# Two gate pairs moved behind the last attention scores, with earlier output weights split over DVE and POOL

## The chip, the core and the metric

The kernel runs on one NeuronCore of a Trainium2 chip. The metric is the device time of one launch in microseconds (us), taken as the median of the runs. The core has five engines that run side by side: TensorE (PE, the matrix array), VectorE (DVE), ScalarE (ACT), GpSimd (POOL) and SyncE (SP, which here only issues DMAs). Each engine works through its own list of instructions in order. An instruction whose operand is not ready stops everything behind it on that engine.

## The reference, cut to what matters

One layer: a norm, one input projection, two mixers on the same normalised input (causal pooling, and latent attention with a mask by chunks of 64 tokens), one output projection, the residual, and a final norm.

```python
u = rmsnorm(h, norm_g) @ w_in
pool_in, pool_gate, c_q, c_kv, k_r, attn_gate = split(u)
pool_out = silu(pool_gate) * pool_mixer(pool_in, pool_w, pool_scale)
q = rmsnorm(c_q) @ w_q_b ; kv = rmsnorm(c_kv) @ w_kv_b
s = (q_nope . k_nope + q_rope . k_rope) * scale      # chunk c sees keys of chunks <= c
attn = softmax(mask(s)) @ v
attn_out = silu(attn_gate) * attn
h = h + concat(pool_out, attn_out) @ w_out
return rmsnorm(h, final_norm_g)[:, 16:]
```

There are 16 meta tokens and 2048 tokens, a model width of 1024, 4 heads, 512 pooling channels and 512 attention channels.

## The kernel before

**Attention.** The 32 chunks of 64 queries are taken one by one in an order written out by hand (`seq`). The stretch that matters here runs over the chunks 19, 18, ..., 8. For a chunk c and a pair of heads p (0 or 1), `scores(c, p)` computes each block of keys with five matmuls into a PSUM bank of the tag "s" (L433 to L437; six such banks). DVE takes the row maxima (L439, L444, L445), ACT the exponentials (L460) and a half-precision copy (L463, L468), DVE or POOL the remainder that the copy lost (L465, L469), and SP issues a DMA that transposes the result into a tile pt (L472), one DMA for each page of keys. `pv(c)` multiplies pt by the values (L496, three matmuls for each tile of keys) into a bank o. It is called one chunk behind the scores: `step(c, 1, 1)` computes the scores of chunk c and then the values of the chunk before it. After four chunks `vproj` (L520, L521) makes an attention tile `at` of 256 tokens.

**The other mixer and the gates.** The 256-token blocks are numbered i = 0 to 7. `load_w(pi)` loads the raw weights of pair pi (L577) and takes their absolute sums on ACT (L580). `scale_w(pi)` finds a power of two by a small matmul (`wmx`, L80) and DVE (L81 to L88), and splits the scaled weights into two half-precision parts (ACT L597, L599, L600; DVE L598; POOL L601). `load_x(i)` does the like for the input of block i (SP L564, DVE L566, ACT L569, POOL L570). `pair(i, pi)` runs two projections of 24 matmuls each (`mproj`, L613) with a gate behind each (ACT L644, L648; DVE L649). Pairs 4 and 5 hold the attention gates (weights 8, 9 and 10, 11), and their result is multiplied into the attention tile on POOL (L702). Pairs 0 to 3 hold a pooling group (`pool_in`: ACT L622, DVE L628, L633, ACT L637 writes `plh`, DVE L638 writes `pll`) and its gate; `pool_out` (three matmuls L658) is put one pair later.

**Output.** `load_wo(k)` loads 128 rows of the output weights (L680) and splits them into a high part (ACT L681) and a low part (DVE L682). `op_prep(t)` makes the two-part operands `mh` (ACT L718, L719) and `ml` (POOL L720, DVE L721) of 128 tokens and loads the residual `xr` (L723). `op(t)` runs 2 x 24 matmuls of 512 columns (L738), adds the residual, norms and stores.

**What sets the order.** The code's own order is a table: `FILL` names the chunks behind which a gate pair is put (after c = 15, 13 and 11, taken from the list `fill` of L805), `PREP` the chunks behind which weights and inputs are loaded, and `TAIL` everything after the attention ("24" is `pair(2, 4)`, "b3" `scale_w(3)`, "o5" `load_wo(5)`, "p0" `op_prep(0)`, "x3" `load_x(3)`). A list scheduler of the framework then merges these into one list for each engine. All raw loads (`raw`, L545: weights, inputs, output weights, residual) share two buffers of one tag, so that a load can be issued when the load two places ahead of it has been used up.

```python
FILL = {15: 1, 13: 1, 11: 1}                                  # L46
return cpools[0].tile([P, cols], F32, name=name, tag="wr", bufs=2, padded_shape=[P, 1088])   # L548
nc.vector.tensor_sub(out=t[:, 1], in0=wr, in1=f(t[:, 0]))     # L682
fill = [(0, 4), (0, 5), (1, 4)]                               # L805
```

## Time and profile before

| | |
|---|---|
| runs | 906.87, 904.96, 903.70 us |
| median | 904.96 us |
| the profiled execution: time, span | 908.45 us, 906.7 us |
| PE busy | 859.5 us (95%) |
| DVE, ACT, POOL busy | 509.3, 455.3, 328.4 us |
| PE idle between 350 and 465 us | 14.07 us |
| PE idle between 465 and 600 us | 7.65 us |
| PE idle between 600 and 850 us | 0 us |

Times inside the execution are counted from the span's start. "Granted clock" is the share of full speed that PE was given: 1.00 is 2.4 GHz, 0.50 is 1.2 GHz. A row of the waits names the waiting instruction, the engine and instruction that it waited for, and how much in total, how often and the longest. In a timeline, the number in brackets at a row's end is the idle time before it and what ended it.

### The profile page before, as it was taken

The page shows a single profiled execution, that of the slowest core. Times are in us where ns is not written, and L with a number is a line of the kernel's source. Part 1 is how long each engine was busy: PE and PEld are TensorE (multiplying, and loading weights), DVE is VectorE, ACT ScalarE, POOL GpSimd, SP SyncE. Part 2 cuts the span into 40 slices and gives each one's busy share as a digit, 9 for nine tenths or more (in the row PEclk, how much of TensorE's full clock was granted, in tenths as well). Part 3 has the DMA queues.
Part 4 walks back from the last instruction along what each step waited for, and adds up shares of the span by engine and source line. Part 5 has one row for each costly group of instructions (what it writes and reads, how often), then busy time and mean ns, then how long its engine had stood idle before and what let it go on. Part 6 is the DMA issues. An engine that isn't in the chain of part 4 may idle for free. (4 is left out here: it accounts for less than half of the span.)

```text
span 906.7 us, 16178 instructions
## 1 busy us (share of the span) xinstructions
PE 859.5 (95%) x5849; PEld 747.1 (82%) x5849; DVE 509.3 (56%) x1224; ACT 455.3 (50%) x1189; POOL 328.4 (36%) x520
## 2 busy tenths in 40 slices
PE   9799899999999999898989997999999999999996
PEld 8699778889888888777878885888888888888885
DVE  5377678756667757768624678454442532534322
ACT  6576657747668667677625554332322312213221
POOL 2566553434545434536413223331312312312020
PEclk9899999999999999998999999999999999999999
DMA  7756525886898788965932234231311312310011
GB/s 267 209 180 176 145 49 103 157 152 131 141 148 146 125 174 138 177 133 141 173 76 74 78 117 145 70 95 72 102 47 47 101 46 64 100 47 1 24 47 70
DMA packets 206955, 101.79 MB, mean 112 GB/s; under 512 B 169257, under 2 KB 196363, under 8 KB 206875
## 3 DMA queue, kind: packets, MB, share of 16 engines
q1 hardware_dynamic: 187392, 93.30, 43.4%
q10 hardware_dynamic: 19483, 7.47, 3.9%
q8 instruction: 46, 0.75, 0.4%
q14 instruction: 34, 0.28, 0.1%
HBM read 55.60 MB, written 8.43 MB: 71 GB/s over the span
## 5 line engine op out<-in xcount | busy, mean ns | idle before, releaser
L613 PEld LDWEIGHTS <-w 128*128 128x128 f16 x2304 | 222.0, 98 | 35.8 <-issue 7.2
L613 PE MATMUL mp<-xx,w 128*128 128x256 f16 x2016 | 233.0, 274 | 0.0
L738 PE MATMUL op<-wo,mh 128*128 128x512 f32 (+1 forms) x528 | 161.3, 388 | 3.1 <-ACT mh L718 3.1
L465 POOL TENSOR_TENSOR hl<-p,hl 128x512 f16<-128x512 f32 (+4 forms) x104 | 102.7, 1008 | 107.0 <-ACT hl L463 102.4
L460 ACT ACTIVATE p<-s,st 128x512 f32<-128x512 f32 (+8 forms) x168 | 99.2, 600 | 52.7 <-DVE st L445 44.0
L738 PEld LDWEIGHTS op<-wo,mh 128*128 128x128 f32 x528 | 97.1, 188 | 23.6 <-ACT mh L718 3.4
L496 PE MATMUL o<-pt,vh 128*128 128x256 f16 x544 | 92.6, 274 | 5.2 <-DMA pt<-hl 4.8
L439 DVE TENSOR_REDUCE st<-s 128x1 f32<-128x512 f32 (+6 forms) x154 | 88.2, 587 | 14.9 <-PE s L437 14.0
L463 ACT CAST hl<-p 128x512 f16<-128x512 f32 (+6 forms) x168 | 82.3, 541 | 5.6 <-DMA pt<-hl 4.3
L740 DVE TENSOR_TENSOR xr<-op,xr 128x512 f32<-128x512 f32 (+1 forms) x33 | 22.2, 674 | 104.3 <-PE op L738 104.3
L496 PE MATMUL o<-pt,vl 128*128 128x256 f16 x272 | 74.5, 274 | 0.0
L742 ACT ACTIVATE osq<-xr 128x512 f16<-128x512 f32 (+1 forms) x33 | 20.4, 618 | 106.7 <-DVE xr L740 97.1
L496 PEld LDWEIGHTS <-vh 128*128 128x128 f16 x544 | 51.9, 98 | 15.1 <-DMA pt<-hl 4.4
L644 ACT ACTIVATE th<-mp,whalf 128x256 f32<-128x256 f32 x64 | 30.1, 471 | 54.4 <-PE mp L613 52.4
L738 PE MATMUL op<-wo,ml 128*128 128x512 f32 x144 | 56.6, 395 | 0.0
L570 POOL TENSOR_TENSOR xx<-yr,xx 128x512 f16<-128x512 f32 x28 | 35.3, 1277 | 45.3 <-ACT xx L569 45.3
L465 DVE TENSOR_TENSOR hl<-p,hl 128x512 f16<-128x512 f32 (+7 forms) x64 | 43.5, 681 | 13.6 <-ACT hl L463 12.5
L433 PE MATMUL s<-klo,qh 128*128 128x512 f32 (+9 forms) x116 | 44.8, 386 | 4.5 <-ACT gt L648 3.4
L623 POOL COPY carry<-u 128x16 f32<-128x16 f32 x32 | 15.2, 475 | 85.2 <-ACT u L622 85.2
L738 PE MATMUL op<-wo,ml_odd 128*128 128x512 f32 (+1 forms) x120 | 45.5, 379 | 0.0
L566 DVE SCALAR_TENSOR_TENSOR yr<-yr,gxs,rbc 128x256 f32<-128x256 f32 (+1 forms) x64 | 32.9, 573 | 21.1 <-DMA yr<-hT_in 17.4
L702 POOL TENSOR_TENSOR at<-at,gt 128x256 f32<-128x256 f32 x32 | 23.5, 734 | 55.7 <-DVE gt L649 45.2
(216 smaller groups left out, 1884.3 us busy)
## 6 DMA issues: line engine op xcount, KB each, us to landing
xt<-hcat_in SPq DMA_DIRECT2D x16, 512.0 KB, 5.3
xr<-hcat_in SPq DMA_DIRECT2D x16, 512.0 KB, 3.6
raw<-hT_in SPq DMA_DIRECT2D x15, 512.0 KB, 5.0
out_dram<-xr SPq DMA_DIRECT2D x15, 512.0 KB, 2.6
yr<-hT_in SPq DMA_DIRECT2D x14, 512.0 KB, 3.7
wr<-w_m_in SPq DMA_DIRECT2D x12, 512.0 KB, 4.5
rb<-rd ACTq DMA_DIRECT2D x32, 128.0 KB, 4.5
wor<-w_out_in SPq DMA_DIRECT2D x8, 512.0 KB, 3.9
```

What stands on the lines that cost most here:

```text
L433: nc.tensor.matmul(ps[:, :w], lhsT=q(qh), rhs=kt[:, 0, 0, sl], start=True, stop=False)
L439: nc.vector.reduce_max(out=mx[:, bi:bi + 1], in_=ps[:, :w], axis=AX.X)
L460: nc.scalar.activation(out=pr[:, o:o + w], in_=pss[bi][:, :w], func=AF.Exp, bias=nb_, accum_out=sm[:, bi:bi + 1] if nb > 1 else tot)
L463: nc.scalar.copy(out=hl[:, 0, sl], in_=pr[:, sl])
L465: eng.tensor_tensor(out=hl[:, 1, sl], in0=pr[:, sl], in1=hl[:, 0, sl], op=ALU.subtract)
L496: nc.tensor.matmul(ps[:, :2 * P], lhsT=v, rhs=x, start=i == 0, stop=i == len(ops) - 1)
L566: nc.vector.scalar_tensor_tensor(out=xr[:, k - k0], in0=xr[:, k - k0], scalar=gxs[:, k:k + 1], in1=rbc, op0=ALU.mult, op1=ALU.mult)
L570: nc.gpsimd.tensor_tensor(out=xl[:, k:k + 2], in0=xr[:, k - k0:k - k0 + 2], in1=xh[:, k:k + 2], op=ALU.subtract)
L613: nc.tensor.matmul(ps[:, :n - sk], lhsT=a[:, k], rhs=x[:, k, sk:n], start=e == 0, stop=e == 3 * KT - 1)
L644: nc.scalar.activation(out=th, in_=ps[:, :G], func=AF.Tanh, scale=whalf[:, wts[m][2]:wts[m][2] + 1])
L702: nc.gpsimd.tensor_tensor(out=t[:, m - 8], in0=t[:, m - 8], in1=gt, op=ALU.mult)
L738: nc.tensor.matmul(ps[:, :w], lhsT=x[:, k], rhs=y[:, sl], start=i == 0, stop=i == 3 * KT - 1)
```

## The change

- The gate pairs (0, 4) and (0, 5) are put behind the chunks 16 and 14 instead of 15 and 13.
- The pair (1, 4) is taken out of the attention loop (it was behind chunk 11), and (1, 5), which was the pair "15" of the tail, joins it: both follow the last scores, with the values of the last chunk, 8, between them.
- In the tail, `scale_w(3)` stands ahead of the pair (1, 1), the output weights 0 to 5 are each loaded one pair sooner, and `op_prep(0)` stands ahead of `load_x(3)` instead of behind the output weights 6.
- The low part of the output weights is made half on DVE (columns 0 to 511) and half on POOL (columns 512 to 1023).

```diff
-FILL = {15: 1, 13: 1, 11: 1}
+FILL = {16: 1, 14: 1}
-TAIL = """b0 w a1 15 24 b1 25 a2 00 10 b2 20 a3 01 11 b3 21 o0 02 o1 12 o2 22 o3 03 o4 13 o5 x3 23 o6 p0 o7 g
+TAIL = """b0 w a1 24 b1 25 a2 00 10 b2 20 a3 01 b3 11 o0 21 o1 02 o2 12 o3 22 o4 03 o5 13 p0 x3 23 o6 o7 g
-        nc.vector.tensor_sub(out=t[:, 1], in0=wr, in1=f(t[:, 0]))
+        nc.vector.tensor_sub(out=t[:, 1, :512], in0=wr[:, :512], in1=f(t[:, 0, :512]))
+        nc.gpsimd.tensor_tensor(out=t[:, 1, 512:], in0=wr[:, 512:], in1=f(t[:, 0, 512:]), op=ALU.subtract)
-    fill = [(0, 4), (0, 5), (1, 4)]
+    fill = [(0, 4), (0, 5), (1, 4), (1, 5)]
+    while fill:
+        pair(*fill.pop(0))
+        if pend:
+            pv(pend.pop(0))
     flush()
-    while fill:
-        pair(*fill.pop(0))
```

In the lists below, `s8_1_1` is the second block of keys of chunk 8 and head pair 1, `o9` the values of chunk 9, `mp1_10` the projection of block 1 with weights 10, `wmx0` the scaling of the tail's first weights, `p15_...` the exponentials of chunk 15.

PE, from the last matmul of the last scores to the scaling of the tail's first weights, before (each row stands for a run of equal rows; weight loads are left out):

```order
L437 MATMUL s8_1_1_6025<-klo_115,qr2_4921 128x336
L613 MATMUL mp1_10_6167<-xx_5318,w10_5150 128x256
L496 MATMUL o10_5963<-pt10_1_5825,vh_120 128x256
L613 MATMUL mp1_11_6197<-xx_5318,w11_5156 128x256
L496 MATMUL o9_6056<-pt9_0_5917,vh_120 128x256
L613 MATMUL mp2_8_6229<-xx_5318,w8_4738 128x256
L496 MATMUL o8_6075<-pt8_0_6006,vh_120 128x256
L496 MATMUL o8_6075<-pt8_1_6014,vh_120 128x256
L613 MATMUL mp2_9_6259<-xx_5318,w9_4744 128x256
L80 MATMUL wmx0_6125<-ident_84,wmx_108 128x128 x4
```

The same place now:

```order
L437 MATMUL s8_1_1_5963<-klo_115,qr2_4982 128x336
L613 MATMUL mp1_8_6013<-xx_5318,w8_4738 128x256
L496 MATMUL o11_5799<-pt11_0_5640,vh_120 128x256
L496 MATMUL o10_5901<-pt10_0_5755,vh_120 128x256
L613 MATMUL mp1_9_6043<-xx_5318,w9_4744 128x256
L613 MATMUL mp1_10_6116<-xx_5318,w10_5212 128x256
L496 MATMUL o9_5994<-pt9_0_5855,vh_120 128x256
L496 MATMUL o8_6075<-pt8_0_5944,vh_120 128x256
L613 MATMUL mp1_11_6146<-xx_5318,w11_5218 128x256
L613 MATMUL mp2_8_6229<-xx_5318,w8_4738 128x256
L80 MATMUL wmx0_6187<-ident_84,wmx_108 128x128 x4
```

The first gate projection of block 1 and the values of chunk 11 have moved behind the last scores. Ahead of the first matmul of `o8` there now stand 57 gate and 53 value matmuls; before, there were 51 and 25. From the last scores to `wmx0` there are 111 gate, 68 value and 12 `av` matmuls; before, 109, 40 and 12.

ACT, around the input cast of block 0 (L569), the exponentials of chunk 15 (L460) and the absolute sums of weights 10 (L580), before:

```order
L597 ACTIVATE w9_4744<-wr9_4593,wsc_104 128x512
L460 ACTIVATE p15_0_0_5015,st15_0_4990<-s15_0_0_4992,st15_0_4990 128x384
L600 CAST w8_4738<-wr8_4587 128x512
L460 ACTIVATE p15_1_0_5064,st15_1_5040<-s15_1_0_5041,st15_1_5040 128x384
L569 CAST x0_4750<-yr0_0_4753 128x544 x2
L580 ACTIVATE wa10_0_4905,wmx_108<-wr10_4903 128x512
L460 ACTIVATE p14_0_0_5241,st14_0_5224<-s14_0_0_5225,st14_0_5224 128x512
```

And now:

```order
L597 ACTIVATE w9_4744<-wr9_4593,wsc_104 128x512
L600 CAST w8_4738<-wr8_4587 128x512
L569 CAST x0_4750<-yr0_0_4753 128x544
L580 ACTIVATE wa10_0_4905,wmx_108<-wr10_4903 128x512
L644 ACTIVATE th0_8_4941<-mp0_8_4915,whalf_106 128x256
L644 ACTIVATE th0_9_4971<-mp0_9_4945,whalf_106 128x256
L460 ACTIVATE p15_0_0_5077,st15_0_5052<-s15_0_0_5054,st15_0_5052 128x384
```

The exponentials of chunk 15 have moved behind the input of block 0, the loads of weights 10 and 11, and the gates of the pair (0, 4).

SP, the raw loads at the end of the output weights, before:

```order
L680 DMA wor5_7284<-w_out_in 128x1024
L564 DMA yr3_0_7290<-hT_in 128x4x256
L564 DMA yr3_4_7300<-hT_in 128x4x256
L680 DMA wor6_7388<-w_out_in 128x1024
L723 DMA xr0_7398<-hcat_in 128x1024
L680 DMA wor7_7401<-w_out_in 128x1024
```

And now:

```order
L680 DMA wor5_7212<-w_out_in 128x1024
L724 DMA xr0_7300<-hcat_in 128x1024
L564 DMA yr3_0_7304<-hT_in 128x4x256
L564 DMA yr3_4_7314<-hT_in 128x4x256
L680 DMA wor6_7402<-w_out_in 128x1024
L680 DMA wor7_7408<-w_out_in 128x1024
```

The residual `xr0` has moved ahead of the two halves of the input of block 3. It keeps its raw buffer until the first output rows are stored, so the four loads behind it take turns in the other one.

## Rows read from the trace of the kernel before

**Rows 1.** Busy time by stretch: length, PE, PEld, DVE, ACT, POOL; clock; DMA share, GB/s.

```profile
650.00:850.00 200.00, 200.00 (x1419) 170.94 (x1418) 80.86 (x167) 53.55 (x123) 46.96 (x74) 1.00 0.17 57
```

**Rows 2.** The same view, ahead of and behind the end of the last scores.

```profile
358.60:447.90 89.30, 79.36 (x576) 70.76 (x575) 65.13 (x170) 61.47 (x172) 44.22 (x58) 0.96 0.77 158
447.90:471.50 23.60, 19.48 (x163) 16.54 (x162) 7.14 (x18) 7.22 (x21) 4.82 (x9) 0.93 0.56 96
```

**Rows 3.** The same view: two stretches of slow clock, and the tail.

```profile
416.00:423.00 7.00, 6.42 (x23) 5.77 (x24) 5.53 (x14) 5.21 (x15) 5.57 (x7) 0.52 0.45 117
...
460.50:464.00 3.50, 3.44 (x18) 2.53 (x19) 0.00 (x0) 0.00 (x0) 0.00 (x0) 0.55 0.26 50
...
500.00:600.00 100.00, 92.35 (x693) 78.03 (x691) 67.69 (x132) 45.67 (x94) 27.61 (x42) 1.00 0.32 99
```

**Rows 4.** PE's waits from 350 to 465 us: total, times, longest.

```profile
PE o L496 <- DMA pt<-hl: 4.1, 1, 4.1
PE s L433 <- ACT gt L648: 3.4, 1, 3.4
```

**Rows 5.** PE's timeline at the last scores: start, length, instruction, count.

```profile
447.49 0.40 PE L437 MATMUL s<-klo,qr 128*128 128x336 f32 x1
...
448.83 4.31 PE L613 MATMUL mp<-xx,w 128*128 128x256 f16 x38
...
454.97 1.47 PE L613 MATMUL mp<-xx,w 128*128 128x256 f16 x12
460.56 0.61 PE L496 MATMUL o<-pt,vh 128*128 128x256 f16 x2 [4.12 <-DMA pt<-hl]
```

**Rows 6.** ACT's timeline from 365 to 452 us, seven rows of it.

```profile
365.35 0.57 ACT L460 ACTIVATE p<-s,st 128x384 f32<-128x384 f32 x1
...
384.70 0.67 ACT L460 ACTIVATE p<-s,st 128x512 f32<-128x512 f32 x1
...
403.65 1.14 ACT L600 CAST w<-wr 128x512 f16<-128x512 f32 x2
...
415.17 0.62 ACT L569 CAST xx<-yr 128x512 f16<-128x512 f32 x1 [0.17 <-DVE yr L566]
...
416.42 0.58 ACT L460 ACTIVATE p<-s,st 128x384 f32<-128x384 f32 x1
...
437.16 0.58 ACT L460 ACTIVATE p<-s,st 128x384 f32<-128x384 f32 x1 [3.33 <-issue]
...
451.11 0.20 ACT L460 ACTIVATION_READ_ACCUMULATOR p<-s,st 128x1 f32 x1
```

**Rows 7.** SP's timeline: half of block 2's input, and the last twelve transposes.

```profile
421.08 0.52 SPq L564 DMA_DIRECT2D yr<-hT_in  x1
...
440.19 17.55 SPq L472 DMA_TRANSPOSE pt<-hl  x12
```

**Rows 8.** PE's waits from 465 to 600 us.

```profile
PE op L738 <- ACT mh L718: 3.1, 1, 3.1
PE pm L658 <- ACT plh L637: 2.1, 1, 2.1
PE wmx L80 <- ACT wa L580: 1.5, 2, 1.1
PE pm L658 <- DVE pll L638: 1.0, 1, 1.0
```

**Rows 9.** Groups on DVE and POOL, 500 to 600 us: count, busy, mean ns, idle.

```profile
L682 DVE TENSOR_TENSOR wo<-wor,wo 128x1024 fp32r<-128x1024 f32 x8 | 9.8, 1223 | 8.8 <-ACT wo L681 8.8
...
L601 POOL TENSOR_TENSOR w<-wr,w 128x512 f16<-128x512 f32 x4 | 4.8, 1200 | 4.0 <-ACT w L600 4.0
```

**Rows 10.** DVE's timeline: a `pl` beside a POOL subtraction, and one without.

```profile
554.26 1.38 DVE L633 SCALAR_TENSOR_TENSOR pl<-w,u 128x256 f32<-128x256 f32 x1
...
561.78 0.42 DVE L633 SCALAR_TENSOR_TENSOR pl<-w,u 128x256 f32<-128x256 f32 x1
```

**Rows 11.** DMA issues, 500 to 575 us: count, size, median us to landing.

```profile
yr<-hT_in SPq DMA_DIRECT2D x2, 512.0 KB, 3.7
```

## The prediction

> **What bounds the kernel now.** I read busy time by stretch first, then PE's waits in the stretches where PE is not full, and last the timelines of the engines that it waits for. From 650 to 850 us PE is busy 200.00 of 200.00 us [rows 1]: there the time is PE's work, the change neither adds nor takes a matmul, and nothing can be won. All that can move is PE's idle time and slow clock ahead of 600 us.
>
> Three terms make that loss. Ahead of the end of the last scores, from 358.60 to 447.90 us, PE is idle 89.30 - 79.36 = 9.94 us, and from 416 to 423 us it runs at a granted clock of 0.52, the lower level of 1.2 GHz, right after a wait of 3.4 us [rows 2 to 4], which costs 7.00 x 0.48 = 3.4 us more: 13.3 us together. Behind the last scores, from 447.90 to 471.50 us (the scaling `wmx0` of the tail's first weights), PE is idle 4.12 us, all of it one wait of `o8` for the transposed softmax of chunk 8 [rows 2, 4, 5], and in the 3.5 us behind that wait its clock is 0.55 [rows 3], which costs 1.6 us: 5.7 us together. In the tail from 500 to 600 us it is idle 100.00 - 92.35 = 7.65 us [rows 3], in four kinds of waits [rows 8].
>
> **The change part by part.** First the two pairs behind the last scores. The need: the last score ends at 447.85 us (the row at 447.49 and its 0.40), and the last page of pt is there when `o8` starts at 460.56 [rows 5]: 12.7 us later. The cover: a gate matmul takes 0.109 us (38 from 448.83 to 452.98, their 4.31 less the overlap with the next [rows 5]), and a value matmul about the same. Before, 51 gate and 25 value matmuls stood between, 76 x 0.109 = 8.3 us; now 57 and 53, 110 x 0.109 = 12.0 us. So 0.7 us of wait is left at most, if the last pages come no later against the last score than now; I take 0.5, and with so short a wait no slow clock (the one of 3.4 us was followed by it). This term falls from 5.7 to 0.5.
>
> What has been moved there is missing ahead. 48 gate and 28 value matmuls are gone from before the last scores, 76 x 0.109 = 8.3 us, and PE's busy time there (79.36 less the 3.4 us of slow clock, 76.0) falls to 67.7. That alone would bring the last scores to 439.6 if the loss of 13.3 us stayed. It does not stay by itself, since the softmax sets the pace. The exponentials of chunk 15 were at 365.35, ahead of block 0's input; in the new list they stand behind it, behind the loads of weights 10 and 11 and behind the gates of (0, 4), all of which used to come behind them. A gate of (0, 4) needs block 0's whole input and 48 matmuls, so I put them at about 383, just ahead of where chunk 14's were (384.70 [rows 6]). From there ACT has one chunk more to do than before. Two things that it did later are already done (the gates of (0, 4) and the absolute sums of weights 10 and 11). The scaling of weights 10 and 11 then ends near 395 instead of 403.65, the first input cast group of block 1 ends 12 us behind it (403.65 to 415.17 [rows 6]), and block 2's, which now stands ahead of chunk 12's exponentials on ACT, another 11 us on: its raw loads need block 1's buffers, and each takes a landing of 3.7 us [rows 11], the scaling on DVE and the casts. So chunk 12's exponentials start at about 418.5, against 416.42 before.
>
> From there on no load is left in between. From 437.16 to 451.31 ACT did three chunks [rows 6] in 14.15 us with three absolute sums of 0.72 each among them, so 4.0 us a chunk; five chunks and the issue of the four reciprocal DMAs (3.3 us [rows 6]) take 23.5 us and end at 442.0. The last exponential ended 3.5 us behind the last score (451.31 against 447.85), so the last score would end at 438.5. PE must stand still for part of this, about 5 us ahead of chunk 11's scores, whose banks wait for chunk 12's exponentials, and the row of 3.4 us says that the lower clock follows: 2 us. With 3.2 us up to 381 (about as now), 1.5 for the scaled weights 10 and 2.0 for the late pt of chunk 15, the loss ahead is 13.7 us, and the last scores end at 358.6 + 67.7 + 13.7 = 440.0. The bounds: 10 us if the slow clock and half of the bank wait do not come (the idle time of now without its slow clock), 20 if block 2's second half is held up as it was before (421.08, behind a transpose on the same queue [rows 7]).
>
> Behind the last scores come 111 gate, 68 value and 12 `av` matmuls, 191 x 0.11 = 21.0, so that `wmx0` stands at 461.5. Before it stood at 471.5 with 46 more gate matmuls done, 5.0 us; on equal work 466.5. **Gain 13.3 + 5.7 - 13.7 - 0.5 = 4.8 us**, bounds -2 and 9.
>
> The tail. `wmx0` now stands 81 gate matmuls ahead of block 0's first pooling projection, 8.9 us, where it stood 35 ahead; so the chain of raw loads (weights 1, 2, 3, then the output weights) runs some 5 us earlier against PE, and the output weights are one pair sooner for that reason, not at a cost. The wait for `mh`, 3.1 us [rows 8], goes: between the two pooling outputs ahead of `op(0)` all 48 matmuls of the pair (2, 3) stand in one piece, 5.2 us, and `mh` is asked for behind them. In its place come others. The casts of output weights 3, 4 and 5 stand on ACT and DVE ahead of block 2's and 0's `plh`: I count 0.7, 3.3 and 1.1 us for the last three `pm` where 2.1 and 1.0 were [rows 8]. The serial raw buffer adds a new pair: input of block 3, first half, second half, output weights 6, 7, each issued only when POOL has finished with the one before, some 7 us a link (3.7 landing [rows 11], DVE 1 to 2, a cast, 1.2 on POOL [rows 9]); 6 is ready about 1.7 us and 7 about 0.7 us behind PE. The scaling waits stay at about 1.2 of 1.5. Sum 8.7 against 7.65: **loss 1.0 us**, bounds -5 and +2 (6 would be the present waits with only the `mh` wait halved; 12.5 if each link is 1.5 us longer).
>
> Splitting the low part: DVE's 1.22 us becomes about 0.65, POOL gets eight times 1.2 [rows 9]. The buffer is free when the slower is done, 1.2 behind the cast as before, so nothing is won on the chain, and POOL (27.61 of 100 us busy [rows 3]) has room. But a `pl` that ran beside a POOL subtraction took 1.38 us, and one without it 0.42 [rows 10]; that may make single links longer and is in the bound above. The Trainium skill's page "SBUF — State Buffer" (section "Who interferes with whom") says that a DVE instruction with two SBUF inputs and a GpSimd instruction that reads SBUF exclude each other for their whole length. By that rule, which speaks against this split and which the 1.38 us agrees with, DVE's and POOL's halves would run one after the other, 1.85 us instead of 1.22, about 0.6 us on each of the three links up to block 3's input, and the sum of the tail would be a loss of some 3 us instead of 1.
>
> Together 4.8 - 1.0 = 3.8 us: 908.45 becomes 904.65. The profiled execution lies 3.5 us (0.4%) above the median of 904.96; the difference carried over to the median gives 901.2.
>
> **The rivals.** *The whole gap goes.* If block 1's and 2's inputs come through as fast as their engines allow, the loss ahead is 10 us and not 13.7, and the tail stays at 7.65: 8.7 us gained, 896. For it: ACT is busy only 61.47 of 89.30 us there, DVE 65.13 [rows 2], so neither is full. Against it: the loads and the softmax stand in one list, and every landing stops the exponentials behind it.
>
> *Exchange.* The wait in front of `o8` comes back ahead, or part of it stays: the last twelve transposes took 17.55 us of SP's queue, 1.46 each [rows 7]. From 420.5 on twenty are due and two weight loads, 30 us, the last landing near 454, while PE reaches `o8` at 440.0 + 12.0 = 452.0. With 2 us left there, and 15 instead of 13.7 ahead, the gain is 2.0 and the tail takes 1.0: 904.
>
> *Slower.* One mechanism: chunk 12's exponentials wait on ACT for the last cast of block 2, in a list that cannot be overtaken. Each of its two halves can be issued only when POOL has freed the buffer, behind whatever stands on SP. If that is 8 us later than I count, the last scores end at 448; on equal work the tail starts 448 + 21.0 + 0.5 - 466.5 = 3.0 us late, plus 1.0 from the tail, and an idle stretch of over 10 us ahead brings 1 us more of slow clock: 5 us lost, 910. It decides once the last scores end after 444, four us behind my figure, with the tail's 1.0 counted.
>
> That the change does not do what it says is no rival: the order of instructions shows both pairs behind the last scores.
>
> **How the numbers follow.** A difference under about 0.3%, 2.7 us, can't be told from no change here. Forecast 0.45, 901.2 with an own range of 899 to 904, a quarter of it inside the 0.3%; whole gap 0.17, 896; exchange 0.16, 904; slower 0.22, 910. Faster 0.34 + 0.17 = 0.51; same 0.11 + 0.16 = 0.27; slower 0.22. The range runs from 895 to 909.5, which leaves out the lower part of the second case and half of the last, about 0.2.
>
> **What would show it.** Right: the wait of `o8` for pt under 1 us and no clock of 0.55 behind it; chunk 15's exponentials near 383, chunk 12's near 418, last scores near 440; no wait for `mh`, new waits of `op` for output weights 6 and 7 (L681), longer `pm` waits. Wrong: last scores after 444, a wait at `o8` over 2 us, a wait of over 3 us in the scores of chunks 13 to 8 in more than one place, or raw loads of the output weights more than 7 us apart on each buffer.

## The result, and the profile after

The change makes the kernel slower: 911.52 us (median of 12 runs) against 906.50 us, ratio 1.0055, interval 1.0035 to 1.0076, so about +5 us where -3.8 us was forecast. The profiled executions are 911.58 and 908.45 us, a difference of 3.1 us; single executions of one kernel differ by several us here, so ratios carry the verdicts and the traces the reasons. A difference of two ratios below is uncertain by about 0.3%.

Two views of the changed kernel answer to [rows 2] and [rows 4]: busy time by stretch (length, PE, PEld, DVE, ACT, POOL; clock, DMA share, GB/s), cut at the end of the last scores (443.30) and at `wmx0` (468.23), with a stretch in which PE mostly stands (418 to 422) and the slow clock behind it; then PE's waits from 350 to 470 us.

```profile
358.44:443.30 84.86, 72.82 (x499) 63.78 (x498) 64.88 (x163) 56.95 (x154) 42.37 (x53) 0.94 0.71 146
443.30:468.23 24.93, 21.25 (x193) 18.60 (x191) 7.83 (x23) 11.11 (x35) 6.17 (x13) 1.00 0.74 140
418.00:422.00 4.00, 1.14 (x7) 0.81 (x6) 4.00 (x6) 3.84 (x11) 4.00 (x4) 1.00 0.12 33
422.00:426.00 4.00, 2.81 (x10) 2.20 (x10) 4.00 (x13) 2.15 (x6) 4.00 (x4) 0.60 0.94 180
```

```profile
PE s L433 <- ACT p L460: 5.2, 3, 2.9
PE o L496 <- DMA pt<-hl: 3.7, 2, 2.8
PE qt L361 <- POOL qra L357: 1.8, 1, 1.8
```

Ahead of the last scores PE is idle 12.0 us and loses 84.86 x 0.06 = 5.1 us more to the clock (some 0.9 us of that fall into idle time and are counted twice): 17.1 us, where 13.3 were before. Behind them it is idle 3.7 us with no slow clock, where 5.7 us were lost. The wait for pt [rows 4, 5] was to go; 3.7 of 4.1 us of it are still there. New are 5.2 us of waits of the scores for exponentials (1.1 us in the kernel before).

What it waits for is on SP. SP's timeline: the two halves of block 2's input, then the transposes and two weight loads up to the last one; and the two rows of PE that wait for the two pages of chunk 8.

```profile
409.49 3.90 SPq L564 DMA_DIRECT2D yr<-hT_in  x2
...
420.92 23.59 SPq L472 DMA_TRANSPOSE pt<-hl  x16
444.56 1.05 SPq L577 DMA_DIRECT2D wr<-w_m_in  x2
446.03 11.64 SPq L472 DMA_TRANSPOSE pt<-hl  x8
```

```profile
458.24 0.39 PE L496 MATMUL o<-pt,vh 128*128 128x256 f16 x2 [2.81 <-DMA pt<-hl]
...
460.70 0.39 PE L496 MATMUL o<-pt,vh 128*128 128x256 f16 x2 [0.87 <-DMA pt<-hl]
```

From 420.92 to 457.67 SP does nothing but 24 transposes and two loads: 1.47 us for each transpose, without a gap. The last ones end at 457.7; before, the last row of twelve ended at 440.19 + 17.55 = 457.7 too [rows 7]. The matmuls were moved, the end of this queue was not. ACT's timeline shows why 24 were due, those of chunks 13 to 8: chunk 15's exponentials are at 386.75, chunk 13's at 414.22, behind block 1's input, and chunk 12's at 421.15. In the kernel before (the last row here) chunk 13's were at 395.98, ahead of that input.

```profile
386.75 0.58 ACT L460 ACTIVATE p<-s,st 128x384 f32<-128x384 f32 x1 [0.29 <-DVE st L445]
...
414.22 0.69 ACT L460 ACTIVATE p<-s,st 128x512 f32<-128x512 f32 x1 [2.53 <-DMA rbc<-rd]
...
421.15 0.59 ACT L460 ACTIVATE p<-s,st 128x384 f32<-128x384 f32 x1
```

```profile
395.98 0.69 ACT L460 ACTIVATE p<-s,st 128x512 f32<-128x512 f32 x1 [1.60 <-DVE st L445]
```

In the tail the wait for `mh` [rows 8] is gone. PE's waits from 470 to 650 us, and the clock behind the longest:

```profile
PE pm L658 <- ACT plh L637: 3.3, 2, 3.0
PE op L739 <- ACT wo L681: 1.5, 2, 1.3
PE pm L658 <- DVE pll L638: 1.2, 1, 1.2
PE op L739 <- POOL wo L683: 0.2, 1, 0.2
```

```profile
547.00:550.00 3.00, 2.55 (x17) 2.09 (x18) 1.87 (x5) 1.25 (x3) 0.40 (x2) 0.84 0.26 91
550.00:555.00 5.00, 5.00 (x36) 3.88 (x33) 4.91 (x8) 2.29 (x6) 4.44 (x3) 0.75 0.12 21
```

The waits are 6.2 us in all where 7.7 were, but behind the wait of 3.0 us at 547.45 the clock falls to 0.84 and 0.75, 3.00 x 0.16 + 5.00 x 0.25 = 1.7 us; before, the clock was 1.00 there [rows 3]. Rows of DVE, POOL and PE up to that wait:

```profile
540.15 0.69 DVE L682 TENSOR_TENSOR wo<-wor,wo 128x512 fp32r<-128x512 f32 x1 [1.39 <-ACT wo L681]
...
540.76 1.52 DVE L628 TENSOR_TENSOR w<-u 128x287 f32<-128x287 f32 x1
```

```profile
540.20 1.78 POOL L683 TENSOR_TENSOR wo<-wor,wo 128x512 fp32r<-128x512 f32 x1 [3.04 <-ACT wo L681]
```

```profile
546.54 0.41 DVE L633 SCALAR_TENSOR_TENSOR pl<-w,u 128x256 f32<-128x256 f32 x1
```

```profile
547.45 0.39 PE L658 MATMUL pm<-plh,pwh 128*128 128x256 f32 x1 [2.98 <-ACT plh L637]
```

POOL's half begins at 540.20, beside DVE's half, and ends at 541.98; DVE's next operation with two inputs takes 1.52 us, where the same operation takes 0.45 in kernel 3 below, which has nothing on POOL there, and ends 0.3 us behind POOL. So the two halves and the operation behind them run one after another: 0.69 on DVE, some 1.1 more on POOL, then DVE again. Each of the six weights that came ahead of 547 us held DVE up by about a microsecond in this way, some half a microsecond more than the half of the subtraction that it was spared, and DVE's `pl` at 546.54 is what the wait goes back to.

### The profile page after: what moved, and what is told of

It is laid out like the page before. It is cut to its first block, busy times and chain, and to the rows that moved or that the text cites. A ratio compares the mean times of both kernels' runs of the same rounds, so it can differ in the third digit from the quotient of the medians.

```text
span 909.8 us, 16209 instructions
## 1 busy us (share of the span) xinstructions
PE 864.2 (95%) x5849; PEld 749.2 (82%) x5849; DVE 515.5 (57%) x1224; ACT 456.9 (50%) x1189; POOL 342.4 (38%) x528
## 5 line engine op out<-in xcount | busy, mean ns | idle before, releaser
L613 PE MATMUL mp<-xx,w 128*128 128x256 f16 x2016 | 230.5, 274 | 0.0
L460 ACT ACTIVATE p<-s,st 128x512 f32<-128x512 f32 (+8 forms) x168 | 99.4, 601 | 53.0 <-DVE st L445 45.0
L741 DVE TENSOR_TENSOR xr<-op,xr 128x512 f32<-128x512 f32 (+1 forms) x33 | 22.3, 675 | 101.8 <-PE op L739 101.8
L496 PEld LDWEIGHTS <-vh 128*128 128x128 f16 x544 | 52.1, 98 | 14.9 <-DMA pt<-hl 4.2
L465 DVE TENSOR_TENSOR hl<-p,hl 128x512 f16<-128x512 f32 (+7 forms) x64 | 45.6, 712 | 17.4 <-ACT hl L463 16.8
L435 PE MATMUL s<-klo,ql 128*128 128x512 f32 (+9 forms) x116 | 43.1, 371 | 0.0
```

Of the source, the lines that this page charges most:

```text
L435: nc.tensor.matmul(ps[:, :w], lhsT=q(ql), rhs=kt[:, 0, 0, sl], start=False, stop=False)
L460: nc.scalar.activation(out=pr[:, o:o + w], in_=pss[bi][:, :w], func=AF.Exp, bias=nb_, accum_out=sm[:, bi:bi + 1] if nb > 1 else tot)
L465: eng.tensor_tensor(out=hl[:, 1, sl], in0=pr[:, sl], in1=hl[:, 0, sl], op=ALU.subtract)
L496: nc.tensor.matmul(ps[:, :2 * P], lhsT=v, rhs=x, start=i == 0, stop=i == len(ops) - 1)
L613: nc.tensor.matmul(ps[:, :n - sk], lhsT=a[:, k], rhs=x[:, k, sk:n], start=e == 0, stop=e == 3 * KT - 1)
```

## Experiments

All ratios are against the kernel before, from runs on the same chip. R is the time from the scaling matmul `wmx` near 358 us to `wmx0`, T the time from `wmx0` to the end of the span. Kernels with the old attention half have 46 gate matmuls more done at `wmx0`; their R is given 5.0 us less and their T 5.0 us more, so that the same work is compared. R and T are of one profiled execution each, and show a change of a few us only roughly: the kernels with the old attention half alone spread over 1.3 us in R, those with nothing but the last two pairs at the end over 3.1.

| | kernel | ratio (interval) | R | T |
|---|---|---|---|---|
| | before | 1 | 107.2 | 440.2 |
| | changed | 1.0055 (1.0035 to 1.0076) | 109.8 | 441.6 |
| 1 | attention half | 1.0024 (1.0004 to 1.0045) | 110.4 | 439.2 |
| 2 | tail half | 1.0040 (1.0017 to 1.0063) | 108.5 | 442.4 |
| 3 | changed, low part on DVE | 1.0010 (0.9988 to 1.0032) | 110.3 | 436.5 |
| 4 | changed, first two pairs back | 1.0030 (1.0009 to 1.0050) | 107.2 | 442.4 |
| 5 | before, POOL half alone | 1.0040 (1.0014 to 1.0067) | 107.8 | 443.7 |
| 6 | 3 with a free POOL operation | 1.0023 (1.0001 to 1.0044) | 112.8 | 440.0 |
| 7 | 3 with half transposes | 0.9954 (0.9931 to 0.9977) | 107.6 | 438.4 |
| 8 | 3 and 4 together | 0.9952 (0.9930 to 0.9974) | 109.6 | 435.6 |
| 9 | tail's list alone | 1.0016 (0.9995 to 1.0038) | 108.1 | 440.8 |
| 10 | 3, six transposes on ACT's queue | 1.0165 (1.0136 to 1.0195) | 129.3 | 433.6 |
| 11 | 8, the same | 1.0098 (1.0068 to 1.0127) | 122.4 | 435.6 |
| 12 | 8 with the tail's old list | 0.9946 (0.9925 to 0.9966) | 106.5 | 436.7 |
| 13 | 12, second pair a chunk sooner | 1.0042 (1.0013 to 1.0071) | 115.2 | 436.3 |
| 14 | 12, first pair a chunk sooner | 1.0038 (1.0012 to 1.0063) | 112.7 | 440.0 |
| 15 | 12, four transposes twice | 1.0037 (1.0015 to 1.0059) | 113.6 | 435.1 |

**1 and 2: the two halves.** 1 has `FILL`, the list `fill` and the loop of the change, 2 its `TAIL` and POOL's half. The fence shows a part of the edits: 1 also has the low part whole on VectorE, 2 the old list `fill` and loop, with "15" kept in `TAIL`.

```diff
 # 1, against the changed kernel
-b2 20 a3 01 b3 11 o0 21 ... o5 13 p0 x3 23 o6 o7 g
+b2 20 a3 01 11 b3 21 o0 ... o4 13 o5 x3 23 o6 p0 o7 g
 # 2, against the changed kernel
-FILL = {16: 1, 14: 1}
+FILL = {15: 1, 13: 1, 11: 1}
```

> The half of the change that moves the gate pairs, alone: FILL, the fill list and the loop behind the chunks as in the changed kernel; the tail's list as before (only 15 gone from it, since that pair is computed earlier) and the low part whole on VectorE. Theory A (the loss sits here: chunk 15's softmax comes behind the gates of (0, 4) and block 0's input, all later transposes of the softmax stand behind the loads of blocks 1 and 2 and are then issued at 1.47 us each, so the wait of o8 stays and the waits in the scores grow): +3 to +5 us against before, a wait of o8 for pt of 2.5 to 4 us, last scores at 443 to 444. Theory B (the loss sits in the tail: POOL's half of the low part and the single raw buffer): -2 to +1 us here; the region still ends with wmx0 at 468, the tail's waits are those of before, 7.7 us or less, and the clock stays up behind 500.

> The other half alone: the tail's list of the changed kernel (with 15 kept in it behind a1, where it was) and the low part half on POOL; the attention half as before. Theory A: within 1 us of before. Theory B: +2.5 to +4 us; the wait of pm for plh of about 3 us near 547 with a clock below 1.00 behind it, and the waits of op for output weights 6 and 7 of 0.2 to 1.7 us. If the two halves only add, this run and the attention half together give the changed kernel's +5.0.

The attention half costs 2.2 us (0.24%), the tail half 3.6 (0.40%). Together 0.64% against 0.55 (0.35 to 0.76) of the whole change: within the intervals they add, and neither theory alone holds. In 1 the wait of `o8` is 2.87 and 0.72 us, as in the changed kernel, and R as long, as theory A had it, though the time is below its 3 to 5 us; the waits of the tail fall to 3.8 us and T is 1 us shorter. In 2 the one wait of about 3 us for `plh` that theory B expected came as two, the longer 1.6 us.

**3: the low part whole on VectorE.**

```diff
-nc.vector.tensor_sub(out=t[:, 1, :512], ...)
-nc.gpsimd.tensor_tensor(out=t[:, 1, 512:], ...)
+nc.vector.tensor_sub(out=t[:, 1], in0=wr, in1=f(t[:, 0]))
```

> The changed kernel with the low part of the output weights whole on VectorE again (one tensor_sub of 1024 columns, nothing of it on POOL). Theory B1 (POOL's half holds up VectorE: its operations behind it take 1.5 us instead of 0.44, five or six times ahead of 547 us, and the chain of raw buffers is longer by it): 1 to 2.5 us faster than the changed kernel, the wait of pm for plh falls from 2.98 to under 1.5 us and the slow clock behind it goes. Theory B2 (the order of the casts, not POOL, makes that wait): within 0.7 us of the changed kernel, the wait stays at 2.5 to 3 us.

0.45% (4 us) faster than the changed kernel, more than expected. DVE's timeline at the same place, the whole subtraction and the operation behind it:

```profile
540.11 1.23 DVE L682 TENSOR_TENSOR wo<-wor,wo 128x1024 fp32r<-128x1024 f32 x1 [1.25 <-ACT wo L681]
...
541.25 0.45 DVE L628 TENSOR_TENSOR w<-u 128x287 f32<-128x287 f32 x1
...
545.41 0.41 DVE L633 SCALAR_TENSOR_TENSOR pl<-w,u 128x256 f32<-128x256 f32 x1
```

DVE is free at 541.7, with all of the weight done, where with POOL's help it is free at 542.3. The `pl` that the long wait went back to stands 75.4 us behind `wmx0` instead of 78.3. The wait of 2.98 us for `plh` is 0.39, no slow clock follows, and T is 5.1 us shorter.

**5 and 6: POOL's half alone, and a POOL operation that nobody waits for.** 5 is the kernel before with the two lines of the change for the low part; 6 is kernel 3 with

```diff
 nc.vector.tensor_sub(out=t[:, 1], in0=wr, in1=f(t[:, 0]))
+dum = cpools[1].tile([P, 512], F32, ...)
+nc.gpsimd.tensor_tensor(out=dum, in0=f(t[:, 0, 512:]), in1=f(t[:, 0, :512]), op=ALU.subtract)
```

> The kernel before with one edit: the second half of the low part of each output weight on POOL, as in the changed kernel. Nothing moves in the attention and in the tail's list. Theory B1 (while POOL's subtraction of 128 x 512 runs, 1.77 us, VectorE's next operation with two inputs is held up: 1.5 instead of 0.44 us): +2 to +4 us against before, waits of pm for plh and pll of over 5 us in all where 3.1 were, and some clock below 1.00 behind them. Theory B2 (only the new order of the output weights makes the loss, the split alone is harmless, as the prediction had it): within 1 us of before.

> The changed kernel with the low part whole on VectorE, and one more POOL subtraction of 128 x 512 fp32 for each of the eight output weights, which reads the finished high part and writes a scratch tile. No raw buffer and no other instruction waits for it. Theory B1 (POOL's subtraction itself blocks VectorE): 2 to 4 us slower than the same kernel without it (907.5), near the changed kernel, with VectorE's operations beside it at 1.5 us again. Theory B3 (POOL costs because it frees the raw buffer 0.55 us later on each link of the chain of loads): within 0.8 us of the kernel without it.

5 loses 3.6 us, by the split and nothing else. Of what was expected in it the waits of `pm` came to 4.6 us, not over 5, the clock did not fall, and 3.0 us of new waits of `op` for output weights came on top: the load of the eighth weight is issued 38.25 us behind that of the first, where it was 35.55. Its DVE row is that of the changed kernel:

```profile
547.03 1.51 DVE L628 TENSOR_TENSOR w<-u 128x271 f32<-128x271 f32 x1
```

6 loses 0.13% (1.2 us) against 3 by the ratios, below the 2 to 4 us of B1 and not clear of no loss at all. Its trace shows the blocking by an operation that frees no buffer: POOL's row, DVE's row that ends 0.3 us behind it, and PE's wait for `plh`, back from 0.39 to 2.56 us.

```profile
526.05 2.31 POOL L684 TENSOR_TENSOR dum<-wo 128x512 f32<-128x512 f32 x1 [1.13 <-ACT wo L681]
```

```profile
527.14 1.50 DVE L633 SCALAR_TENSOR_TENSOR pl<-w,u 128x256 f32<-128x256 f32 x1
```

```profile
547.84 0.58 PE L658 MATMUL pm<-plh,pwh 128*128 128x256 f32 x1 [2.56 <-ACT plh L637]
```

It also shows the longer chain of loads: the eight output weights are issued over 46.6 us, as in the changed kernel (46.5), where it is 42.7 in 3; POOL reads no raw buffer of theirs in 6, so that it is DVE, held up, that frees them later. So the blocking makes the wait and the longer chain without POOL freeing any buffer; that it makes the whole loss of 4 us in time is not shown, since 6 does not lose that much.

**4, 8, 9 and 12: the pairs and the list, apart.** 4 puts `FILL` to `{15: 1, 13: 1}` in the changed kernel, so that (0, 4) and (0, 5) stand where they were and (1, 4) and (1, 5) behind the last scores; 8 is 4 without POOL's half; 12 is 8 with the old list of the tail; 9 is the new list alone, without POOL's half.

> The changed kernel with the first two pairs, (0, 4) and (0, 5), back behind chunks 15 and 13 where they were; the last two pairs still stand at the end between the last scores and the last value products, and the tail is that of the changed kernel. Theory A: chunk 15's exponentials are back near 365 and the transposes are done earlier against the scores, so that the wait of o8 is under 1.5 us and the region wins 3 to 4 us on equal work; with the tail's loss the time is 2 to 4 us below the changed kernel. If the two pairs at the end are themselves the cause (fewer matmuls ahead for the softmax to hide behind, transposes 1.47 us each the bound), the wait stays at over 2.5 us and the time within 1 us of the changed kernel.

> The changed kernel with the low part whole on VectorE and the first two pairs, (0, 4) and (0, 5), back behind chunks 15 and 13; the last two pairs stay at the end, and the tail keeps the changed list. On equal work the region up to the tail's first scaling was the same as before with these two pairs put back (107.2 us), and the tail without POOL's half lost 3.6 us in waits where 6.2 were. Theory B1 with A: 904 to 906 us, 0.5 to 2.5 us below before. Rival (the two gains do not add, since PE reaches the tail 2 us sooner and its chains of loads do not): 906.5 to 908, waits of the tail grown by what the region won.

> The changed list of the tail alone (o0 to o5 and p0 a unit sooner), with 15 kept behind a1, the low part whole on VectorE and the attention half as before. POOL as the cause of the tail's loss: within 1 us of before; the wait for mh, 3.1 us, is gone, and waits of op for output weights 6 and 7 of about 1 us each are there. The list as a cause too: +1.5 us or more against before. The list as a gain of its own: 1.5 us or more below before.

> The last two pairs at the end and the first two where they were, with the tail's old list (only 15 gone from it) and the low part whole on VectorE: what is left of the change when the late softmax of chunk 15, the new list and POOL's half are all taken out. If the two pairs at the end are a gain by themselves: 2 to 5 us below before, 902.5 to 905.5, and the changed list then adds nothing or up to 2 us more. If the gain needs the list: within 1.5 us of before.

12 is 4.9 us below before and 8 is 4.4 (by the ratios, 8 a little better than expected): both beat both kernels. The two pairs behind the last scores are a gain, and the new list adds nothing to it (8 against 12) nor alone (9, within the interval of no change). In 9 the wait for `mh` fell to 0.6 us, and one of 1.4 us for an output weight came. The first two pairs moved a chunk up cost 0.78% (1 against 12), 0.58% (3 against 8) and 0.25% (changed against 4, not clear of nothing by itself). POOL's half costs 0.45% (changed against 3), 0.78% (4 against 8), 0.40% (5) and 0.24% (2 against 9, not clear either). 4 is at the low end of its expectation, 2.3 us below the changed kernel; its waits of `o8` are 1.33 and 1.37 us, and its T, with POOL's half, is 442.4 (435.6 in 8).

Where 12 gains was not where I had put it. Its R, 106.5, is within 1 us of before, and the mean of 4, 8 and 12, 107.8, is that of the four kernels with the old attention half, 107.9. The windows of 12 ahead of the last scores and behind them, and of 8 ahead of them:

```profile
359.50:443.30 83.80, 72.12 (x504) 64.59 (x502) 62.87 (x163) 57.99 (x160) 41.36 (x53) 0.95 0.78 161
443.30:465.90 22.60, 22.10 (x196) 19.46 (x195) 8.07 (x22) 9.22 (x30) 6.59 (x13) 0.98 0.65 126
```

```profile
357.35:444.98 87.63, 73.23 (x503) 65.26 (x503) 63.20 (x163) 58.29 (x161) 42.74 (x55) 0.93 0.78 158
```

Behind the last scores of 12 only 0.5 us is idle and 0.5 lost to the clock: the gap of 5.7 us is filled. Ahead of them 11.7 us is idle and 4.2 lost to the clock, 15.9 where 13.3 were, and in 8 it is 14.4 and 6.1, 20.5: much of what the gap gives back, or more, the stretch ahead loses. A part of this is the same wait in another place, as the *exchange* rival had it: PE waits for pt in front of an earlier chunk's values, 2.20 us in 12 and 4.52 us in 8 (first rows below), and the clock is 0.50 behind both. Another part does not look like the change's: from 396.5 to 400 the clock is 0.51 in 12 and was 1.00 before, behind waits that both kernels have (the last two rows, 12 and before); what decides it is not shown.

```profile
439.77 0.39 PE L496 MATMUL o<-pt,vh 128*128 128x256 f16 x2 [2.20 <-DMA pt<-hl]
```

```profile
440.40 0.61 PE L496 MATMUL o<-pt,vh 128*128 128x256 f16 x2 [4.52 <-DMA pt<-hl]
```

```profile
396.50:400.00 3.50, 3.50 (x18) 2.84 (x18) 2.73 (x11) 2.64 (x8) 1.06 (x2) 0.51 0.00 0
```

```profile
396.50:400.00 3.50, 3.40 (x30) 3.06 (x31) 3.42 (x11) 3.29 (x12) 1.06 (x2) 1.00 0.06 12
```

In these executions the gain is in T, 436.7 for 440.2: PE's waits in the tail of 12 are 4.4 us where 7.7 were.

```profile
PE op L738 <- ACT mh L718: 2.4, 1, 2.4
PE pm L658 <- ACT plh L637: 1.6, 1, 1.6
PE wmx L80 <- ACT wa L580: 0.3, 1, 0.3
```

The wait of the scaling for the absolute sums fell from 1.5 [rows 8] to 0.3, and the waits of `pm` from 3.1 to 1.6: with two more gate pairs done ahead of PE's first output of the tail, `wmx0` and all loads behind it run 5 us earlier against PE. Of the 3.5 us this places 3.3, but 1.7 us of slow clock behind 550 us stand against it, so that a part of T's gain has no row. T of the other kernels with both pairs at the end, the old list and no POOL half (1, 13, 14, 15) runs from 435.1 to 440.0: the gain in time is shown, its place in T is not more than likely.

**7: half of the columns.** In chunks 13 to 8 only the high half is transposed; the low part of these chunks' softmax is left out of the result. The fence shows a part of the edit: it applies to these chunks alone, whose tile `hl` has its low part last, and the value products read the high half twice.

```diff
-last_tr[0] = nc.sync.dma_start_transpose(out=pts[c][pg][3][:, p], in_=hf).ins
+last_tr[0] = nc.sync.dma_start_transpose(out=pts[c][pg][3][:, p, :k], in_=hf[:, :k * P]).ins
```

> The changed kernel with the low part whole on VectorE, and in chunks 13 to 8 only the high halves of the softmax are transposed: 24 transposes as before, each with about half of the columns; the value products read the high half twice, so that TensorE's work stays, but the low part of these chunks' softmax is left out of the result. Theory A (the queue of transposes, 1.47 us each, sets when the last pt lands, and its time is that of the bytes): 0.8 us or less for each, the last pt lands 8 us or more earlier against the first transpose of chunk 13, the wait of o8 falls from 3.5 to under 0.5 us, and 3 to 6 us are won against the kernel without it (907.5). Theory A2 (the time of a transpose is fixed): still 1.4 to 1.5 us each, wait and time as before it. Theory A3 (the exponentials set the pace, the queue only follows): the transposes get shorter with gaps between them, the wait stays at 2 us or more and less than 1.5 us is won.

Theory A's price was wrong, A2's right, though not its forecast of an unchanged time. The group of SP's 24 transposes, in the changed kernel (first) and here, with the shortest, median and longest:

```profile
L472 SPq DMA_TRANSPOSE pt<-hl x24: 1209/1244/2082, 420.9 to 455.6; - x24
```

```profile
L478 SPq DMA_TRANSPOSE pt<-hl x24: 1178/1194/2081, 418.1 to 453.6; - x24
```

Half of the columns take 1194 ns instead of 1244: the time of a transpose on this queue is nearly fixed. The kernel is still 0.56% faster than 3. Its transposes do not wait for the low parts, so that chunk 13's first is issued 59.8 us behind the scaling at 358.3 instead of 63.1 behind that of 3, and PE has the last page 2.7 us earlier (100.0 against 102.7): the start of the queue and the count of its entries set its end. The profiled run shows 2.7 us in R, but lost 1.9 of them again in T and is the slowest of its twelve; the rest of the 5 us I cannot place.

**10 and 11: another queue.** `nc.scalar` instead of `nc.sync` for the second halves of chunks 11, 10 and 9.

> The changed kernel with the low part whole on VectorE, and six of the 24 transposes of chunks 13 to 8 (second halves of chunks 11, 10 and 9) issued from ScalarE's queue instead of SP's. Theory A' (a transpose takes its queue about 1.45 us whatever its size, and that queue sets when the last pt lands): SP's row of transposes gets 8 us shorter, the last pt lands 4 us or more earlier against chunk 13's first transpose, the wait of o8 falls below 1 us, and 2 to 4 us are won against the kernel without it (907.5), less what ScalarE's own issue costs (six times about 0.5 us). Rival (all queues share the transposing hardware): those on SP take longer while ScalarE's run, the last lands within 1.5 us of where it did, and the time is within 1 us or slower.

> The kernel with the last two pairs at the end, the first two where they were, the changed list and the low part whole on VectorE (903.1 us), with the same six transposes from ScalarE's queue. Theory A': 1 to 3 us faster than it, 900 to 902. Rival: within 1 us of it or slower.

A miss for theory A': 14 and 13 us slower by the ratios (against 3 and 8). The rival had "slower", but for another reason. In 10, SP's last row, SP's wait from 420 to 480 us for other transposes, which the changed kernel does not have, and two rows of ACT:

```profile
447.64 27.73 SPq L472 DMA_TRANSPOSE pt<-hl  x8
```

```profile
SPq L472 <- DMA pt<-hl: 21.6, 4, 6.3
```

```profile
445.21 0.37 ACT L498 CAST oh<-o 128x256 fp32r<-128x256 f32 x1 [12.27 <-issue]
...
460.00 0.37 ACT L498 CAST oh<-o 128x256 fp32r<-128x256 f32 x1 [8.57 <-issue]
```

In the program the transposes of two queues wait for each other's landing, so that SP's last eight took 3.5 us each with their waits and ACT, which holds the exponentials, stood 12.3 and 8.6 us in front of its own. The Trainium skill asks for this order (page "Advanced Engine Details and Errata", section "X-Bar Transpose (TRN2)"): transposes of two streams must not be in flight together. The trace shows what the order costs, not what would come without it. The run says nothing on theory A'.

**13, 14 and 15: which pair, and the queue.** 13 has `FILL = {15: 1, 14: 1}`, 14 has `{16: 1, 13: 1}`; 15 issues chunk 11's four transposes a second time:

```diff
 last_tr[0] = nc.sync.dma_start_transpose(out=pts[c][pg][3][:, p], in_=hf).ins
+if c == 11:
+    last_tr[0] = nc.sync.dma_start_transpose(out=pts[c][pg][3][:, p], in_=hf).ins
```

> As the kernel with the last two pairs at the end, the first two where they were, the old list and no POOL half (900.9 us), but the second pair, (0, 5), one chunk sooner, behind chunk 14, as the change has it; the first stays behind chunk 15. If it is the first pair that costs (chunk 15's softmax, which it puts off, sets when all later transposes can go): within 1.5 us of 901. If it is the second (block 1's loads then stand ahead of chunk 13's transposes): 905 to 908, with 22 to 24 transposes still due when block 1's second half is issued.

> The other one: the first pair, (0, 4), behind chunk 16 as the change has it, the second behind chunk 13 where it was. If the first pair costs: 905 to 908, chunk 15's exponentials near 385 instead of 365. If the second: within 1.5 us of 901. If only both together do: each of these two near 903 to 904.

> The kernel of 900.9 us with chunk 11's four transposes issued twice (the same page written again), so that SP's queue has four more, about 5.9 us at 1.47 each, and nothing else is moved on purpose. If the queue of transposes sets when the last pt lands: it lands 4 to 6 us later against the first scaling at 358, PE waits for pt by 3 to 5 us more, and the time is 903.5 to 906. If the exponentials set it and the queue has slack: the last pt within 2 us of before, the time within 1.5 us of 901.

All three lose the gain of 12 and some 4 us more; either pair alone costs as much as both, which none of the readings had. SP's last row of transposes in 12, 13 and 14, with fourteen entries in 12 and sixteen in the others, and the wait of `o8` in 12, 13, 14 and 15:

```profile
433.38 22.70 SPq L472 DMA_TRANSPOSE pt<-hl  x14
```

```profile
435.83 24.38 SPq L472 DMA_TRANSPOSE pt<-hl  x16
```

```profile
431.65 24.29 SPq L472 DMA_TRANSPOSE pt<-hl  x16
```

```profile
456.94 0.39 PE L496 MATMUL o<-pt,vh 128*128 128x256 f16 x2 [0.50 <-DMA pt<-hl]
```

```profile
464.09 0.60 PE L496 MATMUL o<-pt,vh 128*128 128x256 f16 x2 [4.53 <-DMA pt<-hl]
```

```profile
459.67 0.39 PE L496 MATMUL o<-pt,vh 128*128 128x256 f16 x2 [4.63 <-DMA pt<-hl]
```

```profile
461.33 0.39 PE L498 MATMUL o<-pt,vh 128*128 128x256 f16 x2 [2.15 <-DMA pt<-hl]
```

The rows of `o8` are those of the first of its two pages. Counted from the scaling near 358, PE has this page at 97.5 us in 12 and 96.7 in 4, at 104.3, 101.8 and 104.6 in 13, 14 and 15, at 100.5 in 1, at 99.8 in the changed kernel and at 101.3 before. In 15 the four added entries are worth 7.1 us at that place and 0.91% (8 us) of time, more than the 5.9 us of their own queue time: the list scheduler also put one weight load behind the added transposes (446.15 us, in 12 432.76), and waits of the scaling of 1.9 us came back. So what is put into the queue of transposes is paid at the last value products.

For the first pairs this is a part of the cost and not all of it: the page is 3.0 us later in 1 than in 12, and the time 7 us longer. Nor is the queue the only thing that makes the page late. Its last transpose is issued by 96.6 us in 12, by 100.5 in 13, 98.0 in 14 and 101.7 in 15, and from issue to landing the transposes from 450 to 458 us take 2.7 us (median) in 12 and 4.3, 6.1 and 4.2 in those. What makes the landing longer is not shown. Why one pair costs as much as two is not settled either: 13 also has a wait of 4.0 us of the scores for exponentials, 14 one of 3.5 us for DVE and, in the tail, one of 5.4 us for `mh`.

## Why the prediction was wrong, step by step

Two steps failed: what the first two pairs, put a chunk sooner, do to the softmax behind them (the wait at `o8` and the loss ahead), and POOL's half, priced at nothing. Without both, and with the tail's old list, the kernel gains 4.9 us (12).

- **The wait at `o8`**, 0.5 us in the sum, was 3.7. I kept the need of 12.7 us behind the last score fixed ("if the last pages come no later against the last score than now"). It was 458.24 - 443.30 = 14.9 us, and 0.87 more for the second page. (The 12.7 was read from a row of the first of `o8`'s two pages; "the last page" was a misreading, since PE asked for the second one later and did not wait.) The cover of 12.0 us was right: PE came to `o8` at 458.24 - 2.81 = 455.43, 12.1 us behind the last score. A queue that runs on its own does not end earlier because PE has done its scores earlier. With the first two pairs back, in 12, the need is 13.7 and the wait 0.5.
- **The exchange** rival had this mechanism, its start (420.5, measured 420.92) and its price (1.46, measured 1.47), but counted twenty transposes. Twenty-four were due, since chunk 13's also stood behind block 1's input, and 24 x 1.47 + 1.05 = 36.3 us end at 457 and land 3 us later, at 460, where I had 454. With this count it would have had 8 us left at `o8` instead of 2, and a loss.
- **The loss ahead**, 13.7 us, was 17.1, and the last scores ended at 443.3, not 440.0. PE's work there was right within a microsecond: 72.82 - 5.1 = 67.7 us, as forecast. Chunk 15's exponentials were 3.8 us later than I put them, chunk 12's 2.7 us. The wait of the scores was 5.2 us for 5; the 2.0 for a late pt of chunk 15 did not come, but 2.5 for weights 10 came where I had 1.5, and 5.1 us of slow clock where I had 2, a part of it behind those weights. The *slower* rival, which had the delay of chunk 12 and came nearest by its number, decided too late ("after 444"): the wait at `o8` was charged on top, which I had ruled out there.
- **POOL's half**, in the sum at nothing, cost 1.6 to 6.8 us of T in its four pairs of kernels, and 0.24 to 0.78% of the time. "POOL has room" was the wrong question. The 1.38 us row [rows 10] was in the bound and should have been the price: 1.5 for 0.45 us each time. The rule of the Trainium skill (page "SBUF — State Buffer", section "Who interferes with whom") that I weighed had the mechanism, which the traces agree with (DVE's operation ends 0.3 us behind POOL's). Its price in the prediction, a tail loss of 3 us instead of 1, was half of the 4 us measured against kernel 3.
- **No slow clock behind `o8`**: 1.00 in the profiled run, but by luck, since the reason given was a wait of 0.5 us and it was 2.8.
- **Region**: gain 4.8 forecast; R is 2.6 us longer. That 12 gains 4.9 in time is near the forecast by luck too: its R is only 0.7 us shorter.
- **Tail**: loss 1.0 forecast, T 1.4 us longer: the sum was right by luck. The wait for `mh` went, and waits for output weights 6 and 7 came (1.7 us for 2.4 forecast); `pm` waited 1.2, 3.0 and 0.3 us for 0.7, 3.3 and 1.1. But POOL's half was not in it, nor a gain from the earlier loads (3.5 us of T in 12's execution), which I had only called not a cost.

## What to carry to other kernels

A gap in front of a wait is filled with other work only if the chain behind the wait keeps its own time: count the entries of its slowest queue from where it last stood still, and take that as the end. Ask also what work put sooner between the producers of that chain pushes back; here the two pairs put a chunk sooner cost as much as the two pairs put behind the last chunk gained, or more (0.58 and 0.78% without POOL's half, against 0.54%). Half of an operation on POOL is not half of its time if DVE reads two inputs meanwhile.

## What the runs showed of the hardware

- A transpose of a softmax page takes SP's queue 1.19 to 1.24 us (median) with two to four blocks of 128 columns as with four to eight, 1.47 us with what stands between two of them. From issue to landing it takes a median of 2.7 us in 12 and 6.1 in 14, at the same place.
- POOL's subtraction of 128 x 512 from two inputs takes 1.77 us beside a DVE one of 0.69 us, and a DVE operation with two inputs that starts under it takes 1.5 us instead of 0.45. Where POOL's starts first (528.81 us in the changed kernel), it takes 1.27 us and DVE's half 1.72.
- The clock did not follow the length of a wait alone: behind a wait of 2.98 us at 547 it was 0.75 to 0.84, behind one of 2.81 us at 458 it stayed at 1.00, and behind one of 2.86 us at 421.88 it fell to 0.60. Behind two short waits that both kernels have ahead of 397 us it was 1.00 in the kernel before (1.66 and 0.43 us) and 0.51 in 12 (1.36 and 0.41 us).
